# First block's attention: both maps' score products on 64-row halves of TensorE, written alternately, from one split of the queries

## The chip, the cores and the metric

The kernel runs on one core of a Trainium2 chip. The metric is the time of the whole program in device microseconds, a median over runs. The kernel before takes 3630.28 us (median of 3 runs).

## What is computed

The reference applies two transformer blocks of two layers each to 512 tokens of width 1024. The change touches one place: layer 0 of the first block, whose mixer is a differential attention over 8 heads. Each head has two maps (c = 0 and 1), each with queries and keys of width 64, and one set of values of width 128. The 512 latent tokens are the queries; the keys and values are those of 512 latent and 256 context tokens, 768 in all:

```python
def diff_attn_core(q, k, v, lam):
    s = jnp.einsum('bqhcd,bkhcd->bhcqk', q.astype(jnp.float32), k.astype(jnp.float32))
    p = jax.nn.softmax(s * (1.0 / math.sqrt(HEAD_DIM)), axis=-1)
    a = p[:, :, 0] - lam * p[:, :, 1]
    return jnp.einsum('bhqk,bkhe->bqhe', a.astype(v.dtype), v)
```

Each head's output is normed over its 128 channels and goes into the output product.

## The kernel before

The program is one long list of instructions for five engines. Its order on each engine is set when it is built, by a planner that lists instructions by its own estimates of when operands and buffers come free; on the chip each engine takes its list in order and waits with semaphores. All products with weights run in three passes: an operand is split into a high and a low part (float32r) that add up to it, and high x low, high x high and low x high are summed in PSUM (`mm3`, lines 246 to 254). Raw weights come by DMA into `wr`; the split (`split`, lines 221 to 223) writes the high part `wh` on ScalarE and the low part `wl` on VectorE, in 4 buffers each.

The attention stage, `diff_attention`, goes through 32 steps: 8 heads x 4 blocks of 128 queries (qi). QT[h] and KT[h] hold a head's queries and keys feature-major: 128 partitions, rows 0 to 63 for map 0 and 64 to 127 for map 1; columns are tokens (512 and 768). VV holds the values, token-major.

- `prep(h)` (named `after` and `psplit` inside, line 695 for all) makes a head's operands on GpSimd alone, one instruction after the other. `ks` is the pair of high and low keys. The high queries go into a `wh` buffer of the weights, twice: copy c is multiplied by a mask (`halves`) that is 0 on the other map's 64 rows. `qlo` is the low part of the queries.
- `scores(h, qi)` makes one map after the other. A map takes a PSUM tile `s` of two banks (768 columns used; three such tiles, s=3) and six products (line 723): the masked high queries against low and high keys, on all 128 rows, and the low queries against the high keys, on the map's 64 rows; each in a piece of 512 and one of 256 columns. Then VectorE takes the negative maximum over the keys (line 725), and ScalarE the exponential into `pp` with the row sum (line 727), which frees the tile.
- `mix(h, qi)`, one step later, joins the two maps on VectorE (lines 735 to 737), transposes the result on TensorE (line 746, tile `tr`, two banks) and copies it to `aT` on ScalarE (line 748).
- `values(h, half)` (line 757) multiplies with VV for two steps at a time; `finish_a` and `finish_b` sum squares (line 301), take the power on GpSimd (line 314), spread it (line 296), scale on VectorE (line 779) and split the head's output into `Oh` and `Ol`.

Ahead of the stage stands `qkv`, whose last products (the second half of the values) end in copies to VV on ScalarE (line 654). Behind it stands the output product with the weights `wo`.

Of the kernel before, what the change touches and what calls it, by code (L numbers as in the profile page):

```python
# [10 lines left out]
F32 = mybir.dt.float32  # L11
# [7 lines left out]
P = 128  # L19
# [9 lines left out]
# columns of the packed feature-major vectors  # L29
# [19 lines left out]
# columns of the packed row vectors  # L49
# [15 lines left out]
class Seg:  # L65
    """a run of tokens: columns lo..lo+w of x(k) for feature chunk k, columns off..off+w of the split activations"""
# [11 lines left out]
class Part:  # L78
    """tokens that share a PSUM bank in a product, and the segments that norms take one after the other"""
# [5 lines left out]
class Ps:  # L85
    """PSUM pool with a number of buffers per tag"""
# [8 lines left out]
class RmsMod:  # L95
    """rms norm with gain, scale and shift, into the split activations H"""
# [10 lines left out]
    def ahead(self, xn, seg, r=None):  # L107
        """normed values without gain and shift"""
        pr = self.net.row_bcast(self.sums(seg) if r is None else r)
        for k in range(KD):  # L110
            self.net.V.tensor_tensor(xn[:, k, seg.cols()], seg(k), pr, ALU.mult)
        self.early[seg.off] = xn
# [31 lines left out]
class LayerNorm:  # L144
    """layer norm of the stream in place, and its split in H (or each chunk handed to out)"""
# [27 lines left out]
class Net:  # L173
# [16 lines left out]
    def phase(self, ctx, name, tbufs, reuse="tile"):  # L190
        """open the scratch pool of a phase"""
        self.pool = ctx.enter_context(self.tc.tile_pool(name=self.nm(name), bufs=1, reuse_waits=reuse))
        self.tbufs = tbufs
# [20 lines left out]
    # ---- weights: raw float32 in, split into two float32r parts that add up to it  # L214
# [21 lines left out]
    def units(self, src, ks, n):  # L236
        """ks blocks of n columns, as many per unit as fit"""
# [8 lines left out]
    def mm3(self, outs, lhs, start, stop):  # L246
        """outs: list of (psum, rhs hi, rhs lo); lhs: (hi, lo)"""
# [13 lines left out]
    def later(self, steps, work):  # L261
        """have work done behind that many steps of products"""
        self.pending.append((self.steps + steps, work))

    def product(self, outs, lhs):
        """outs: list of (psum, k -> rhs hi, k -> rhs lo); lhs: list over k of (hi, lo)"""
# [4 lines left out]
    def constant(self, dst, rows, one, eng=None):  # L271
        """fill rows of a float32r tile [p, m, n] with 0 or 1"""
        (eng or self.G).memset(dst[rows].bitcast(F32), float(one))

    # ---- small vector arithmetic
# [17 lines left out]
    def bcast(self, dst, cols):  # L293
        """dst psum [128, 128*n]: row vector of cols[128 tok, n] on every partition"""
# [3 lines left out]
    def col_sums(self, dst, x):  # L298
        """dst psum [128 tok, n]: sums over the partitions of x [128, n*128 tok]"""
# [11 lines left out]
    def pow_half(self, dst, v):  # L311
        """dst = v ** -0.5 on GpSimd"""
# [17 lines left out]
    def row_ln(self, acc, accq, w, n):  # L330
        """rstd and mu*rstd per token, on every partition; sums over n channels"""
# [22 lines left out]
    # ---- setup  # L354
    def setup(self):
# [17 lines left out]
        self.halves = cp.tile([P, 2], F32, name="halves")  # L373
        nc.vector.memset(self.halves, 0.0)
        for c in range(2):
            nc.vector.memset(self.halves[64 * c:64 * c + 64, c:c + 1], 1.0)
# [17 lines left out]
    # ---- the nine modulation vectors of a layer, for one or both conditions  # L394
# [47 lines left out]
    def fill(self, n):  # L442
        """advance the pending modulation vectors by n steps"""
# [16 lines left out]
    def norm_scale(self, l, i, msc):  # L460
        """g * (1 + scale) for norm i of layer l: [128, 8, 2]"""
# [7 lines left out]
    # ---- product that ends in the stream: weights stationary, one unit list per chunk of output features.  # L469
    # The last chunks go segment by segment, so that the norm of one segment runs beside the product of the next.  # L470
# [21 lines left out]
    # ---- gated feed-forward on the split activations H  # L492
# [79 lines left out]
    # ---- first block, layer 0: differential attention  # L572
    def head_rope(self, pt, G, out, tabs):
        """pt psum [128, G*64] -> out: rms norm over 64, gain and rotation folded in the tables"""
# [18 lines left out]
    def rotate(self, src, cosg, sing, o3, q):  # L593
        """src [128, G, 4q]; pairs are (0,q), (2q,3q) blocks; sing holds -sin first, +sin second"""
# [11 lines left out]
    def rope_tables(self, cos, sin, g, w, tiles, scale=1.0):  # L606
        """cos [128, 4, w], sin signed; g [128, w]: tables with the gain folded in"""
# [21 lines left out]
    def qkv(self, H, QT, KT, VV):  # L629
        """queries and keys normed, rotated, feature-major; values token-major; context tokens are tiles 4 and 5"""  # L630
# [52 lines left out]
    def diff_attention(self, QT, KT, VV, O, keep):  # L683
        """O[h]: split feature-major outputs of head h. p0 - lam*s0/s1*p1 stands for the attention; the factor 1/s0 of
        each query goes into the norm over the head's channels: 1/s0 / sqrt(ms/s0^2 + eps) = 1/sqrt(ms + eps*s0^2)."""
# [5 lines left out]
        prev = []  # L691

        def after(*args):
            with self.tc.issue_after(prev.pop()) if prev else nullcontext():
                prev.append(G.tensor_tensor(*args).ins)

        def psplit(dst, src):
            one = self.ones[:, :1] if len(src.shape) == 2 else self.ones[:, :1].unsqueeze(1)
            after(dst[0], src, one.to_broadcast(list(src.shape)), ALU.mult)
            after(dst[1], src, dst[0].bitcast(F32), ALU.subtract)  # L700

        def prep(h):
            k = self.pair("ks", [P, NK], 2)
            psplit(k, KT[h])
            qh = self.wp.tile([P, 1024], F32R, name=self.nm("wh"), tag="wh", bufs=4).rearrange("p (c t) -> p c t", c=2)
            qlo = self.tile([P, T], "qlo", 2, F32R)
            for c in range(2):
                b = slice(64 * c, 64 * c + 64)
                after(qh[:, c], QT[h], self.halves[:, c:c + 1].to_broadcast([P, T]), ALU.mult)
                after(qlo[b], QT[h][b], qh[b, c].bitcast(F32), ALU.subtract)  # L710
            heads[h] = dict(qh=qh, qlo=qlo, k=k, s0=self.small(4, "s0", 3))

        def scores(h, qi):
            d = heads[h]
            ql = slice(qi * P, qi * P + P)
            d["p", qi], rr = [], (d["s0"][:, qi:qi + 1], self.small(1))
            for c in range(2):
                b = slice(64 * c, 64 * c + 64)
                st = self.bank("s", 1024)
                qh, qlo, (kh, kl) = d["qh"][:, c, ql], d["qlo"][b, ql], d["k"]  # L720
                for lh, r, on in ((qh, kl, (True, False)), (qh, kh, (False, False)), (qlo, kh[b], (False, True))):
                    for c0, c1 in ((0, 512), (512, NK)):
                        PE.matmul(st[:, c0:c1], lh, r[:, c0:c1], start=on[0], stop=on[1])
                nmax = self.small(1)
                V.tensor_reduce(nmax, st[:, :NK], axis=AX.X, op=ALU.max, negate=True)
                p = self.tile([P, NK], "pp", 6)
                S.activation(p, st[:, :NK], AF.Exp, bias=nmax, accum_out=rr[c])
# [73 lines left out]
    # ---- first block, layer 1: Fourier mix on half spectra  # L801
# [74 lines left out]
    # ---- second block  # L876
    def proj_tm(self, us, n, H, tt):
        """token-major product of token tile tt"""
# [12 lines left out]
    def mixer(self, l, H, norm):  # L891
# [19 lines left out]
        # attention operands per pair of heads: queries and keys feature-major, one head per block, then a row that  # L911
        # takes minus the maximum of each query (ones on the side of the keys); values token-major with ones between
# [604 lines left out]
```

## Time and profile before

| | |
|---|---|
| median of 3 runs (lowest, highest) | 3630.28 us (3626.2, 3633.18) |
| span of the profiled execution | 3633.2 us |
| TensorE products, busy share of the span | 94% |
| TensorE weight loads | 78% |
| VectorE | 57% |
| ScalarE | 35% |
| GpSimd | 14% |
| attention stage, first score product to first product with wo | 812.65 to 990.34 us |

The profiled execution's span lies at the upper end of the runs. Busy shares are means over stages that differ, so the stage is read for itself: a table of stretches gives the busy time of each engine in it, the waits say who ended whose idle time, and the timeline gives starts and durations. A product's duration in the timeline includes its way through the array, so products overlap in it; what a product costs in a row of products is the distance from start to start.

### The profile page before, as it was taken

How to read it: one execution, taken by the hardware profiler on the slowest of the kernel's cores; microseconds unless marked ns; L12 is line 12 of the kernel's file. 1: busy time of each engine (PE TensorE's matmuls, PEld its weight loads, DVE VectorE, ACT ScalarE, POOL GpSimd, SP SyncE). 2: the span in 40 equal slices, each digit the busy share in tenths (PEclk: the TensorE clock that was granted, in tenths of full speed). 3: DMA queues.
4: the chain of work that ended last, by engine and by line, in shares of the span. 5: the costliest groups of instructions: out<-in, count | busy, mean ns of one | idle time of the engine just before them, and what ended most of it. 6: DMA issues, size and time to landing. Idle time of an engine off the chain costs nothing.

```text
span 3633.2 us, 44413 instructions
## 1 busy us (share of the span) xinstructions
PE 3425.2 (94%) x17540; PEld 2839.1 (78%) x17540; DVE 2084.7 (57%) x3447; ACT 1267.5 (35%) x2180; POOL 517.0 (14%) x481
## 2 busy tenths in 40 slices
PE   7999999999999999999999999669999994999998
PEld 5888888777787778888888888557888873688887
DVE  6554355667664555333463336985744679666556
ACT  3211214336542224222452224235533441554333
POOL 1000001015410001000120003740100049020001
PEclk9999999999999999999999999879999996899999
DMA  6343352120045563333223333101333320023232
GB/s 222 122 141 112 101 161 72 50 70 1 24 154 160 181 195 123 99 95 97 74 99 93 93 98 91 41 21 47 93 95 97 93 80 14 18 70 110 90 102 64
DMA packets 99449, 341.80 MB, mean 94 GB/s; under 512 B 10916, under 2 KB 14116, under 8 KB 98984
## 3 DMA queue, kind: packets, MB, share of 16 engines
q1 hardware_dynamic: 99240, 338.96, 30.0%
q8 instruction: 138, 2.26, 0.3%
q14 instruction: 71, 0.58, 0.1%
HBM read 336.82 MB, written 2.10 MB: 93 GB/s over the span
## 4 chain that ended last, share of the span: by engine, by line
PE 35%; issue 6%; DVE 5%; POOL 4%; ACT 1%; ACTq 0%; DVEq 0%; POOLq 0%
PE mm L250 12%; PE mm L254 11%; PE mm L252 11%; POOL yb L1261 2%; POOL cx L1259 1%; DVE wl L223 1%; DVE ya L1255 0%; DVE s L290 0%; DVE s L291 0%; DVE s L289 0%; DVE t L164 0%; DVE t L165 0%; ACT H L222 0%; POOL s L314 0%; ACT X L166 0%
## 5 line engine op out<-in xcount | busy, mean ns | idle before, releaser
L222 ACT ACTIVATE wh<-wr 128x1024 fp32r<-128x1024 f32 (+4 forms) x505 | 510.9, 1014 | 1364.3 <-PE mm L252 894.2
L250 PE MATMUL mm<-H,wh 128*128 128x512 f32 (+1 forms) x2592 | 968.0, 374 | 11.6 <-DVE nm L1119 5.8
L254 PE MATMUL mm<-H,wl 128*128 128x512 f32 (+1 forms) x2592 | 963.0, 372 | 1.5 <-DVE wl L223 1.4
L252 PE MATMUL mm<-H,wh 128*128 128x512 f32 (+1 forms) x2592 | 964.2, 372 | 0.0
L223 DVE TENSOR_TENSOR wl<-wr,wh 128x1024 fp32r<-128x1024 f32 (+4 forms) x505 | 602.5, 1194 | 445.5 <-ACT wh L222 435.7
L250 PEld LDWEIGHTS mm<-H,wh 128*128 128x128 f32 x2592 | 494.6, 191 | 103.5 <-DVE nm L1119 6.5
L254 PEld LDWEIGHTS mm<-H,wl 128*128 128x128 f32 x2592 | 493.9, 191 | 85.8 <-DVE wl L223 2.3
L252 PEld LDWEIGHTS mm<-H,wh 128*128 128x128 f32 x2592 | 495.0, 191 | 83.5 <-issue 0.5
L254 PE MATMUL mm<-ah,wl 128*128 128x512 f32 (+1 forms) x1216 | 445.9, 367 | 0.0
L252 PE MATMUL mm<-ah,wh 128*128 128x512 f32 (+1 forms) x1216 | 443.8, 365 | 0.0
L250 PE MATMUL mm<-al,wh 128*128 128x512 f32 (+1 forms) x1216 | 443.1, 365 | 0.0
L252 PEld LDWEIGHTS mm<-ah,wh 128*128 128x128 f32 x1216 | 228.3, 188 | 42.4
L250 PEld LDWEIGHTS mm<-al,wh 128*128 128x128 f32 x1216 | 228.3, 188 | 42.3 <-issue 1.2
L254 PEld LDWEIGHTS mm<-ah,wl 128*128 128x128 f32 x1216 | 228.7, 188 | 39.5
L419 DVE SCALAR_TENSOR_TENSOR macc<-wr,SC,macc 128x1024 f32<-128x1024 f32 x133 | 168.3, 1281 | 94.3 <-DMA wr<-w_mod 93.7
L568 DVE SCALAR_TENSOR_TENSOR X<-mm,ng,X 128x512 f32<-128x512 f32 (+1 forms) x120 | 81.3, 678 | 244.8 <-PE mm L254 244.7
L314 POOL TENSOR_TENSOR s<-s,mhalf 128x2 f32<-128x2 f32 (+1 forms) x26 | 21.0, 806 | 1355.5 <-ACT s L321 816.4
L250 PE MATMUL mm<-wl,H 128*128 128x512 f32 (+2 forms) x480 | 180.7, 378 | 33.7 <-DVE wl L223 30.4
L528 DVE TENSOR_TENSOR act<-act,mm 128x512 f32<-128x512 f32 x88 | 60.3, 686 | 240.0 <-PE mm L254 239.8
L254 PE MATMUL mm<-wh,H 128*128 128x512 f32 (+2 forms) x480 | 176.7, 370 | 0.3
L252 PE MATMUL mm<-wh,H 128*128 128x512 f32 (+2 forms) x480 | 176.4, 368 | 0.0
L156 POOL TENSOR_TENSOR cx<-X 128x512 f32<-128x512 f32 x5 | 9.3, 1851 | 1005.7 <-DVE X L1267 638.2
(348 smaller groups left out, 4921.9 us busy)
## 6 DMA issues: line engine op xcount, KB each, us to landing
wr<-gu SPq DMA_DIRECT2D x176, 512.0 KB, 3.5
wr<-w_mod SPq DMA_DIRECT2D x136, 512.0 KB, 4.2
wr<-up SPq DMA_DIRECT2D x88, 512.0 KB, 3.5
wr<-dn SPq DMA_DIRECT2D x48, 448.0 KB, 3.4
wr<-down SPq DMA_DIRECT2D x32, 448.0 KB, 3.3
wr<-qkv SPq DMA_DIRECT2D x24, 512.0 KB, 4.3
wr<-dn SPq DMA_DIRECT2D x24, 512.0 KB, 3.6
wr<-w_out SPq DMA_DIRECT2D x16, 512.0 KB, 3.5
```

Source lines behind the costliest of these rows:

```text
L156: (net.G if k < KD - 1 else net.V).tensor_tensor(self.acc[:, sl], self.acc[:, sl] if k > 1 else seg(0), seg(k), ALU.add)
L222: self.S.activation(hi, src, AF.Copy)
L223: (eng or self.V).tensor_tensor(lo, src, hi.bitcast(F32), ALU.subtract)
L250: self.PE.matmul(pt, lh, rl, start=start, stop=False)
L252: self.PE.matmul(pt, lh, rh, start=False, stop=False)
L254: last = self.PE.matmul(pt, ll, rh, start=False, stop=stop)
L314: G.tensor_tensor(dst, v, self.mhalf.to_broadcast([P, w]), ALU.pow)
L419: self.V.scalar_tensor_tensor(acc[c], raw, s, acc[c], ALU.mult, ALU.add)
L528: self.V.tensor_tensor(to, to, pu, ALU.mult)
L568: self.V.scalar_tensor_tensor(s(d), pt, gate[0][:, d, s.cond:s.cond + 1], s(d), ALU.mult, ALU.add)
L1259: G.tensor_tensor(x, ap[:, j, t2:t2 + T], wt(t2).to_broadcast([P, T]), ALU.mult)
L1261: G.tensor_tensor(yb[:, j], yb[:, j], x, ALU.add)
```

## The change

The queries are split once, like any other operand: `split` with ScalarE for the high part and GpSimd for the low part, for keys and queries. `qs` is the new pair of queries, with two buffers of its own; the `wh` buffers, the masked copies and `halves` are not used any more. All six products of a map run on its 64 rows, and the code writes those of the two maps alternately, into two PSUM tiles taken together. Maxima and exponentials follow as before. The rest of the diff takes out comments and docstrings.

```diff
         def prep(h):
-            k = self.pair("ks", [P, NK], 2)
-            psplit(k, KT[h])
-            qh = self.wp.tile([P, 1024], F32R, name=self.nm("wh"), tag="wh", bufs=4).rearrange("p (c t) -> p c t", c=2)
-            qlo = self.tile([P, T], "qlo", 2, F32R)
-            for c in range(2):
-                b = slice(64 * c, 64 * c + 64)
-                after(qh[:, c], QT[h], self.halves[:, c:c + 1].to_broadcast([P, T]), ALU.mult)
-                after(qlo[b], QT[h][b], qh[b, c].bitcast(F32), ALU.subtract)
-            heads[h] = dict(qh=qh, qlo=qlo, k=k, s0=self.small(4, "s0", 3))
+            q, k = self.pair("qs", [P, T], 2), self.pair("ks", [P, NK], 2)
+            for dst, src in ((k, KT[h]), (q, QT[h])):
+                self.split(dst[0], dst[1], src, G)
+            heads[h] = dict(q=q, k=k, s0=self.small(4, "s0", 3))
 
         def scores(h, qi):
+
             d = heads[h]
             ql = slice(qi * P, qi * P + P)
             d["p", qi], rr = [], (d["s0"][:, qi:qi + 1], self.small(1))
+            st = [self.bank("s", 1024) for _ in range(2)]
+            half = [slice(64 * c, 64 * c + 64) for c in range(2)]
+            for i, (x, y) in enumerate(((0, 1), (0, 0), (1, 0))):
+                for c0, c1 in ((0, 512), (512, NK)):
+                    for c, b in enumerate(half):
+                        PE.matmul(st[c][:, c0:c1], d["q"][x][b, ql], d["k"][y][b, c0:c1], start=i == 0, stop=i == 2)
             for c in range(2):
-                b = slice(64 * c, 64 * c + 64)
-                st = self.bank("s", 1024)
-                qh, qlo, (kh, kl) = d["qh"][:, c, ql], d["qlo"][b, ql], d["k"]
-                for lh, r, on in ((qh, kl, (True, False)), (qh, kh, (False, False)), (qlo, kh[b], (False, True))):
-                    for c0, c1 in ((0, 512), (512, NK)):
-                        PE.matmul(st[:, c0:c1], lh, r[:, c0:c1], start=on[0], stop=on[1])
                 nmax = self.small(1)
```

The planner orders the instructions of the stage anew. Three places of the built orders follow; the number behind a name tells tiles apart.

ScalarE at the start of the stage, before: the last two VV copies of `qkv`, the table load and small exponential for lambda, then the first exponentials of head 0.

```order
L654 ACTIVATE VV<-mm_6784 128x512
L654 ACTIVATE VV<-mm_6810 128x512
L678 ACT_TABLE_LOAD
L678 ACTIVATE s_6846<-s_6846 128x2
L727 ACTIVATE pp_6877,s_6866<-s_6868,s_6875 128x768
```

The same place after:

```order
L650 ACTIVATE VV<-mm_6780 128x512
L222 ACTIVATE wh_8484<-wr_8482 128x1024
L222 ACTIVATE wh_8517<-wr_8515 128x1024
L222 ACTIVATE wh_8552<-wr_8550 128x1024
L650 ACTIVATE VV<-mm_6806 128x512
L222 ACTIVATE ks_6854<-KT_5124 128x768
L222 ACTIVATE qs_6852<-QT_5116 128x512
L674 ACT_TABLE_LOAD
L674 ACTIVATE s_6842<-s_6842 128x2
L222 ACTIVATE ks_6909<-KT_5125 128x768
L222 ACTIVATE qs_6907<-QT_5117 128x512
L222 ACTIVATE wh_8587<-wr_8585 128x1024
```

Four splits of wo units (wh from wr) have moved here from the last heads, and the high parts of head 0's and head 1's keys and queries stand here, those of head 0 behind the last VV copy.

TensorE in head 1, block 2, before: the two maps (tiles s_7121 and s_7132) follow one another, four products on 128 rows and two on 64 each.

```order
L723 MATMUL s_7121<-ks_6914,wh_6917 128x512
L723 MATMUL s_7121<-ks_6914,wh_6917 128x256
L723 MATMUL s_7121<-ks_6913,wh_6917 128x512
L723 MATMUL s_7121<-ks_6913,wh_6917 128x256
L723 MATMUL s_7121<-ks_6913,qlo_6918 128x512
L723 MATMUL s_7121<-ks_6913,qlo_6918 128x256
L723 MATMUL s_7132<-ks_6914,wh_6917 128x512
```

The same step after:

```order
L703 MATMUL s_7111<-ks_6910,qs_6907 128x512
L703 MATMUL s_7111<-ks_6910,qs_6907 128x256
L703 MATMUL s_7111<-ks_6909,qs_6907 128x512
L703 MATMUL s_7111<-ks_6909,qs_6907 128x256
L703 MATMUL s_7111<-ks_6909,qs_6908 128x512
L703 MATMUL s_7111<-ks_6909,qs_6908 128x256
L703 MATMUL s_7112<-ks_6910,qs_6907 128x512
```

All six products of map 0 (s_7111, upper 64 rows) still stand ahead of those of map 1 (s_7112, lower 64 rows), though the code alternates; every one is on 64 rows now.

TensorE in head 2, blocks 1 and 2, after: s_7257 and s_7258 are the maps of block 1, s_7313 and s_7314 those of block 2, tr_7246 is the spreading of a head's factor (line 296).

```order
L703 MATMUL s_7258<-ks_7079,qs_7077 128x512
L296 MATMUL tr_7246<-ident,or_7154 128x128 x4
L703 MATMUL s_7257<-ks_7079,qs_7077 128x256
L703 MATMUL s_7258<-ks_7079,qs_7077 128x256
L703 MATMUL s_7257<-ks_7079,qs_7078 128x512
L703 MATMUL s_7258<-ks_7079,qs_7078 128x512
L703 MATMUL s_7257<-ks_7079,qs_7078 128x256
L703 MATMUL s_7258<-ks_7079,qs_7078 128x256
L703 MATMUL s_7313<-ks_7080,qs_7077 128x512
L703 MATMUL s_7313<-ks_7080,qs_7077 128x256
```

TensorE in the same head before, from the second map of block 0 (s_7231) to the first of block 1 (s_7267):

```order
L723 MATMUL s_7231<-ks_7085,qlo_7090 128x512
L757 MATMUL tr_7210<-aT_7100,VV 128x256 x6
L723 MATMUL s_7231<-ks_7085,qlo_7090 128x256
L723 MATMUL s_7267<-ks_7086,wh_7089 128x512
L723 MATMUL s_7267<-ks_7086,wh_7089 128x256
```

In the order after, the alternation is kept here, and both maps of block 1 end within one product of each other; before, the maps follow one another, and the six products of a map stand between the end of one and the end of the next.

## Rows read from the trace of the kernel before

**Rows 1.** Stretches: window, us, busy us (instructions) of PE, PEld, DVE, ACT, POOL, clock, DMA

```profile
850.00:890.00 40.00, 39.92 (x197) 28.86 (x196) 29.85 (x41) 24.49 (x57) 21.10 (x21) 1.00 0.00 1
```

**Rows 2.** Groups, 812 to 972 us: operation, count | busy us, mean ns | idle before

```profile
L737 DVE SCALAR_TENSOR_TENSOR pp<-pp,s,pp 128x768 f32<-128x768 f32 x29 | 36.2, 1247 | 0.4
...
L695 POOL TENSOR_TENSOR qlo<-QT,wh 64x512 fp32r<-64x512 f32 x15 | 23.3, 1556 | 1.2
...
L736 DVE SCALAR_TENSOR_TENSOR s<-s,nlam,s 128x1 f32<-128x1 f32 x29 | 17.6, 606 | 0.3
...
L695 POOL TENSOR_TENSOR wh<-QT,halves 128x512 fp32r<-128x512 f32 x15 | 16.5, 1101 | 0.0
...
L695 POOL TENSOR_TENSOR ks<-KT,ones 128x768 fp32r<-128x768 f32 x7 | 10.3, 1467 | 39.2 <-PE s L723 39.1
L223 POOL TENSOR_TENSOR Ol<-t,Oh 128x512 fp32r<-128x512 f32 x6 | 7.7, 1279 | 18.9 <-ACT Oh L222 18.9
```

**Rows 3.** Timeline of TensorE in a burst of maps: start, us, operation, count

```profile
837.85 0.96 PE L723 MATMUL s<-ks,wh 128*128 128x512 f32 x4
838.74 0.61 PE L723 MATMUL s<-ks,qlo 64*128 64x512 f32 x2
839.28 0.96 PE L723 MATMUL s<-ks,wh 128*128 128x512 f32 x4
```

**Rows 4.** Timeline of TensorE, 512- and 256-column products alternating

```profile
300.13 0.40 PE L250 MATMUL mm<-H,wh 128*128 128x512 f32 x1
...
300.49 0.40 PE L252 MATMUL mm<-H,wh 128*128 128x512 f32 x1
...
301.19 0.40 PE L250 MATMUL mm<-H,wh 128*128 128x512 f32 x1
```

**Rows 5.** Timeline of GpSimd, TensorE and ScalarE around the start

```profile
783.99 1.83 POOL L695 TENSOR_TENSOR ks<-KT,ks 128x768 fp32r<-128x768 f32 x1
...
812.65 0.85 PE L723 MATMUL s<-ks,wh 128*128 128x512 f32 x4
812.85 0.60 ACT L654 ACTIVATE VV<-mm 128x512 f32<-128x512 f32 x1 [4.84 <-PE mm L254]
```

**Rows 6.** Waits, 812 to 972 us: who, for whom, us, times, longest

```profile
DVE s L725 <- PE s L723: 33.6, 29, 5.0
...
PEld s L723 <- issue: 24.6, 102, 0.7
...
PEld s L723 <- ACT pp L727: 1.2, 3, 0.7
```

**Rows 7.** Timeline of TensorE, VectorE and ScalarE in the last burst

```profile
965.94 0.75 DVE L779 SCALAR_TENSOR_TENSOR t<-t,subg,tr 128x512 f32<-128x512 f32 x1 [0.57 <-PE tr L296]
966.72 0.63 ACT L222 ACTIVATE Oh<-t 128x512 fp32r<-128x512 f32 x1 [0.33 <-DVE t L779]
967.30 0.61 PE L723 MATMUL s<-ks,qlo 64*128 64x512 f32 x2
967.95 0.96 DVE L725 TENSOR_REDUCE s<-s 128x1 f32<-128x768 f32 x1 [0.32 <-PE s L723]
968.82 0.21 DVE L736 SCALAR_TENSOR_TENSOR s<-s,nlam,s 128x1 f32<-128x1 f32 x1
968.94 0.90 ACT L727 ACTIVATE pp<-s,s 128x768 f32<-128x768 f32 x1 [0.36 <-DVE s L725]
970.27 1.01 DVE L737 SCALAR_TENSOR_TENSOR pp<-pp,s,pp 128x768 f32<-128x768 f32 x1
```

**Rows 8.** Timeline, then a stretch, at the stage's end

```profile
974.13 1.20 DVE L223 TENSOR_TENSOR wl<-wr,wh 128x1024 fp32r<-128x1024 f32 x1
...
989.93 0.65 PE L296 MATMUL tr<-ident,or 128*128 128x128 f32 x4 [1.63 <-POOL or L314]
990.34 0.48 PE L250 MATMUL mm<-Ol,wh 128*128 128x512 f32 x1
...
992.00:994.00 2.00, 2.00 (x6) 1.59 (x5) 0.00 (x0) 0.13 (x1) 1.27 (x1) 0.50 0.00 0
```

More of the change, by code (lines that the diff above doesn't have):

```diff
@@ L372, in setup @@
             nc.vector.memset(t, e)
-        self.halves = cp.tile([P, 2], F32, name="halves")
-        nc.vector.memset(self.halves, 0.0)
-        for c in range(2):
-            nc.vector.memset(self.halves[64 * c:64 * c + 64, c:c + 1], 1.0)
         self.SC = cp.tile([P, KD, 32], F32, name="SC")
@@ L689, in diff_attention @@
         heads = {}
[L691 to L700, printed above, removed]
-        def prep(h):
-            k = self.pair("ks", [P, NK], 2)
-            psplit(k, KT[h])
-            qh = self.wp.tile([P, 1024], F32R, name=self.nm("wh"), tag="wh", bufs=4).rearrange("p (c t) -> p c t", c=2)
-            qlo = self.tile([P, T], "qlo", 2, F32R)
-            for c in range(2):
-                b = slice(64 * c, 64 * c + 64)
-                after(qh[:, c], QT[h], self.halves[:, c:c + 1].to_broadcast([P, T]), ALU.mult)
-                after(qlo[b], QT[h][b], qh[b, c].bitcast(F32), ALU.subtract)
-            heads[h] = dict(qh=qh, qlo=qlo, k=k, s0=self.small(4, "s0", 3))
+        def prep(h):
+            q, k = self.pair("qs", [P, T], 2), self.pair("ks", [P, NK], 2)
+            for dst, src in ((k, KT[h]), (q, QT[h])):
+                self.split(dst[0], dst[1], src, G)
+            heads[h] = dict(q=q, k=k, s0=self.small(4, "s0", 3))
         def scores(h, qi):
@@ L716, in scores @@
             d["p", qi], rr = [], (d["s0"][:, qi:qi + 1], self.small(1))
-            for c in range(2):
-                b = slice(64 * c, 64 * c + 64)
-                st = self.bank("s", 1024)
-                qh, qlo, (kh, kl) = d["qh"][:, c, ql], d["qlo"][b, ql], d["k"]
-                for lh, r, on in ((qh, kl, (True, False)), (qh, kh, (False, False)), (qlo, kh[b], (False, True))):
-                    for c0, c1 in ((0, 512), (512, NK)):
-                        PE.matmul(st[:, c0:c1], lh, r[:, c0:c1], start=on[0], stop=on[1])
+            st = [self.bank("s", 1024) for _ in range(2)]
[4 more added lines that the diff above has]
+                        PE.matmul(st[c][:, c0:c1], d["q"][x][b, ql], d["k"][y][b, c0:c1], start=i == 0, stop=i == 2)
+            for c in range(2):
                 nmax = self.small(1)
-                V.tensor_reduce(nmax, st[:, :NK], axis=AX.X, op=ALU.max, negate=True)
+                V.tensor_reduce(nmax, st[c][:, :NK], axis=AX.X, op=ALU.max, negate=True)
                 p = self.tile([P, NK], "pp", 6)
-                S.activation(p, st[:, :NK], AF.Exp, bias=nmax, accum_out=rr[c])
+                S.activation(p, st[c][:, :NK], AF.Exp, bias=nmax, accum_out=rr[c])
                 d["p", qi].append(p)
```

## Prediction

> **What bounds the kernel now.** I read the table of stretches first: from 812 us to 972 us, the score stage of the first block's attention, TensorE is busy 39.92 of 40 us (850 to 890 stands for the four stretches) while VectorE is at 29.85, ScalarE at 24.49 and GpSimd at 21.10 [rows 1]. So this stage is TensorE's, and a microsecond taken from TensorE there is a microsecond of the kernel, until VectorE (three quarters busy) or a wait takes its place. The waits say the same: VectorE's largest, 33.6 us, is for the score products; TensorE's largest has no releaser, 24.6 us in 102 pieces called "issue" at the scores' weight loads; its wait for a score bank (the exponentials of line 727 give banks back) is 1.2 us in all [rows 6].
>
> What are the 102 pieces? The timeline of TensorE answers. One map of one step is six products: four on 128 rows (wh, against the low and high keys), two on 64 rows (qlo). The four start at 837.85, the two at 838.74, the next map's four at 839.28: 0.89 + 0.54 = 1.43 us a map [rows 3]. Where 512- and 256-column products alternate without a change of rows, six take 300.13 to 301.19 = 1.06 us [rows 4]. The difference, 0.37 us, is two changes between 128-row and 64-row mode: **0.185 us a change**, in which the engine drains and the first load is not hidden. This is the price that the change attacks.
>
> **Part by part.** *Fewer mode changes.* In the new kernel all score products use 64 rows; transposes, values and sums use 128. I counted in the built instruction orders, from the first score product to the last product of the stage: 154 changes of mode before, 107 after (a transpose put between two 128-row products used to be free and now costs two changes, so not all 128 go). 47 x 0.185 = **-8.7 us**, all of it on TensorE's path.
>
> *Alternation.* The code asks for twelve products per step that alternate between the halves. The order does not keep it: of 32 steps, only 8 alternate in a lasting way (step 0 with 11 changes of half, five steps with 8, two with 3 or 4); in the other 24 all six products of map 0 stand ahead of map 1's, since the second bank comes late. In all 95 neighbours change half, 235 stay on one. No row of the trace has two neighbouring products on different halves (the two qlo groups of a step are always parted by wh products), so the price is bounded by the nearest rows: at best each change of half hides a 256-column product, 300.49 - 300.13 = 0.36 us a pair, of which a third is the 256 columns, 0.12 us, so -11.4 us; at worst it costs as much as a mode change, +17.6 us. I take **-2 us**: some overlap, most of it lost because in the same steps TensorE waits (next point). The Trainium skill ("TensorE: Matmul & The Clock Gate", Part 3) says that products on different row groups run at once, about 4 ns apart; by that rule this term is the whole -11.4, and it is my second rival.
>
> *Where alternation survives, a bank is late.* There are three score banks. Before, map 0 ends 1.43 us ahead of map 1, so its maximum and exponential run beside map 1's products. In the 8 alternating steps both maps end together. The next step's map 0 takes the third bank (1.06 us); its map 1 needs the bank of the old map 0: maximum 0.96 us and exponential 0.90 us later, and about 0.1 us for the handovers (products end 967.30 + 0.61 = 967.91, maximum at 967.95 to 968.91, exponential at 968.94) [rows 7] = 1.96 us, so TensorE stands 0.9 us. In five of the eight the broadcast product and its VectorE operation (0.75 us, line 779 [rows 7]) stand just ahead of that maximum, which adds up to 0.3 us. 8 x 1.1 = **+9 us**, against 1.2 us of such waits now [rows 6]. The Trainium skill ("TensorEngine Tiling (Array Packing)", PSUM Bottleneck) warns of just this, that packing speeds up TensorE and not the emptying of PSUM. Bounds: 0, if the other work between hides it, to 8 x 1.96 = 15.7.
>
> *The start.* Before, GpSimd makes head 0's operands without ScalarE: the low keys end at 783.99 + 1.83 and the first score starts at 812.65, straight behind the last projection product [rows 5]. After, ScalarE makes the high parts, and its order puts head 0's ks and qs copies behind the last VV copy, which waits for that last product: it ends at 812.85 + 0.60 = 813.45. Then the 128x768 copy (no such row; the exponential of that size takes 0.90), then the low keys on GpSimd, 1.83 with VectorE idle: 813.45 + 0.90 + 1.83 = 816.2, and one handover. First score 3.6 us later than now, and the low queries (a subtraction of this size takes GpSimd 1.28, the Ol row [rows 2]) hold the last four products until 817.5. I take **+3.8 us**; below 3.0 it can't be, since copy and subtraction are in line.
>
> *Behind the start.* A weight unit's split (1.20 us on VectorE [rows 8]) that stood in the last heads now stands between the second and third maximum, and the second head's two copies ahead of the first exponential. So maps 4 and 6 wait for banks: **+2 us** (0 to 3). TensorE's idle time can also cost clock: at the stage's end it waits 1.63 us, and 992 to 994 runs at 0.50 of the clock (1.2 GHz) [rows 8]. Such a stretch at the new start would fall in waits for banks: **+0.5 us** (0 to 1.7).
>
> *ScalarE and GpSimd.* ScalarE gets 8 x (0.90 + 0.63) = 12.2 us more (the 512-column copy is the Oh row [rows 7]): 24 of 40 us become 27, still far from the bound. GpSimd loses the ones- and halves-products: per head 1.47 + 2 x 1.10 + 2 x 1.56 go, one subtraction of 1.28 comes [rows 2]. That helps VectorE: the p update takes 1.247 on average but 1.01 in a burst with GpSimd idle, the small factor 0.606 against 0.21 [rows 2, 7]. I count nothing for it: VectorE waits for TensorE 33.6 us; at best it trims the bank waits by 2 us. The wh buffers that qh no longer holds let four splits of the next stage go early; the loads' order is the same, and the next stage starts behind the same chain at the tail: nothing.
>
> **Sum**: -8.7 - 2 + 9 + 3.8 + 2 + 0.5 = **+4.6 us**. The profiled execution spans 3633.2 us, at the upper end of the three runs (3626.2 to 3633.18); 3633.2 + 4.6 = 3637.8 in it, and against the median of 3630.28: **3635 us**. One effect, a shift of the free phase of the clock's dips later on, I can't sum: +-2 us.
>
> **Rivals.** *1. A change of half costs like a change of mode* (slower). For it: nothing in the trace shows two halves at work at once. Then +17.6 in place of -2; the slower TensorE hides about 5 us of the bank waits: 4.6 + 19.6 - 5 = +19, 3649 us. It decides from about 0.05 us a change of half on, where 95 x 0.05 + 2 brings the sum above +7.3. *2. Full overlap and hidden waits* (faster): -8.7 - 8 - 0, with 3 of the 9 us of waits, 3.8 and 0: -10, 3620 us. For it: VectorE has 11 us of 40 free, and GpSimd disturbs it less. Against: with both maps ready at once the bank chain of 1.96 us is longer than the one map that covers it. By the rule of the TensorE page named above this is what the tiles would allow. *3. No overlap and no price*: the halves simply follow one another; 4.6 + 2 = +6.6, 3637 us. *4. The clock*: the 3.6 us gap at the start and the waits behind it hold TensorE at 1.2 GHz for longer than one such stretch; twice 1.7 us for it and once more at the tail, +5 on top: 3640 us. That the change does not do what it says is partly built in: 24 of 32 steps don't alternate.
>
> **How the numbers follow.** About 0.2% (7.3 us) is what a measurement of this kernel can tell from no change: 3623.0 to 3637.5 is "same". Forecast 0.42 (its own range 3629 to 3639; 0.37 same, 0.05 slower); rival 1 0.15 (slower); rival 2 0.15 (0.12 faster, 0.03 same); rival 3 0.17 (0.10 same, 0.07 slower); rival 4 0.11 (0.09 slower, 0.02 same). Faster 0.12, same 0.52, slower 0.36. Range 3620 to 3648: it leaves out the far half of rival 1 and what lies beyond rival 2.
>
> **What would show it.** First score product about 816.3 us, not 812.65, with TensorE's wait put on GpSimd. "Issue" at the scores' loads down by about a third. A map that follows on the same half at 1.06 us, not 1.43. In alternating steps, starts of neighbours a few ns to 0.1 us apart (overlap), 0.12 to 0.22 (none) or 0.3 and more (rival 1). Waits of score loads on the exponentials: from 1.2 to about 10 us in the stage; if they stay near 2, rival 2 holds. The stage from 812.65 to the first wo product at 990.34 (177.7 us) [rows 5, 8] should come out at about 182. I am wrong if ScalarE gets at head 0's copies before the last VV copy, or if the bank waits hide under values and transposes.

## The result, and the profile after

The changed kernel takes **3674.47 us** (median of 4 runs, 3673.49 to 3677.72) against 3631.73 for the kernel before on the same chip (4 runs, 3626.2 to 3633.94): ratio 1.0117, 95% interval 1.0104 to 1.0129. It is slower by some 43 us; the forecast was 3635 us, with a range up to 3648. The profiled execution spans 3675.9 us, so the difference to the profiled one of before (3633.2) is 42.7 us as well, and it can be split by three times in the two traces: the first score product, the first product with wo, the end.

| | before | after | difference |
|---|---|---|---|
| up to the first score product | 812.65 | 814.01 | +1.4 |
| from there to the first product with wo | 177.7 | 196.9 | **+19.2** |
| from there to the end of the span | 2642.9 | 2665.0 | **+22.1** |

So there are two losses, one in the stage that was changed and one, just as large, in code that was not touched.

**The stage.** The table of stretches of after, with the columns of [rows 1] (us; busy us and instructions of TensorE, its loads, VectorE, ScalarE, GpSimd; clock; DMA):

```profile
812.00:850.00 38.00, 34.09 (x146) 26.45 (x147) 27.30 (x40) 26.68 (x55) 13.98 (x11) 0.66 0.11 42
850.00:890.00 40.00, 37.70 (x176) 27.86 (x176) 18.75 (x31) 20.06 (x47) 8.13 (x11) 0.85 0.00 0
890.00:930.00 40.00, 35.42 (x186) 26.99 (x185) 26.64 (x39) 24.86 (x56) 12.27 (x14) 0.91 0.00 1
930.00:972.00 42.00, 38.50 (x191) 28.96 (x190) 25.68 (x41) 24.41 (x55) 9.32 (x11) 0.88 0.00 1
972.00:990.00 18.00, 16.88 (x85) 12.39 (x85) 7.43 (x13) 9.62 (x23) 1.21 (x2) 0.85 0.00 1
990.00:1010.00 20.00, 17.23 (x88) 13.74 (x84) 7.34 (x14) 8.84 (x22) 4.87 (x8) 0.88 0.00 1
```

The column to look at is the clock. Before it is 1.00 from 812 to 990 [rows 1]; after it is 0.66 in the first stretch and 0.85 to 0.91 behind it, up to the stage's end at 1010.94. It is a mean of two levels, 2.4 and 1.2 GHz: the engine ran at half speed for two thirds of 812 to 850 us (0.66 = 1 - 0.68/2) and for parts of every stretch. Summed over the rows, (1 - clock) x us is 12.9 + 6.0 + 3.6 + 5.0 + 2.7 + 2.4 (the rows are rounded), some **32 us** of full-speed time lost; before, nothing in the stage.

The waits of the same stage (who, for whom, us in total, times, longest), which answer to [rows 6]:

```profile
DVE s L706 <- PE s L703: 30.3, 16, 6.3
PEld s L703 <- ACT pp L708: 9.5, 8, 1.5
PEld s L703 <- issue: 7.4, 38, 0.3
PE s L703 <- ACT pp L708: 6.9, 7, 1.2
PE s L703 <- POOL ks L223: 3.3, 1, 3.3
```

"Issue" at the score loads fell from 24.6 us in 102 pieces to 7.4 in 38: most of these pieces are gone, as intended, though the order still has 107 of the 154 mode changes. Waits for a PSUM tile rose from 1.2 to 9.5 us (the second line; the fourth tells them from the products' side), and one wait of 3.3 us stands at the start. The timeline of ScalarE, GpSimd and TensorE there, which answers to [rows 5] (start, duration, engine, line, operation):

```profile
811.24 0.83 ACT L222 ACTIVATE ks<-KT 128x768 fp32r<-128x768 f32 x1
```

```profile
812.16 1.80 POOL L223 TENSOR_TENSOR ks<-KT,ks 128x768 fp32r<-128x768 f32 x1 [175.16 <-DMA wr<-wo]
```

```profile
810.32 0.40 PE L254 MATMUL mm<-wh,H 128*128 128x512 f32 x1
814.01 4.20 PE L703 MATMUL s<-ks,qs 64*128 64x512 f32 x18 [3.30 <-POOL ks L223]
```

GpSimd's subtraction for the low keys starts when ScalarE's copy of the high keys has ended (811.24 + 0.83 = 812.07), so that copy is what it waited for; the DMA that the row names brings weights of `wo`, which it doesn't read.

VectorE's and GpSimd's groups answer to [rows 2] (count | busy us, mean ns):

```profile
L718 DVE SCALAR_TENSOR_TENSOR pp<-pp,s,pp 128x768 f32<-128x768 f32 x27 | 32.0, 1185 | 0.5
L717 DVE SCALAR_TENSOR_TENSOR s<-s,nlam,s 128x1 f32<-128x1 f32 x27 | 11.3, 420 | 0.2
L223 POOL TENSOR_TENSOR qs<-QT,qs 128x512 fp32r<-128x512 f32 x8 | 10.2, 1276 | 40.1 <-ACT qs L222 40.1
```

With less work on GpSimd the p update takes 1185 ns instead of 1247 and the small factor 420 instead of 606. It buys nothing, since neither engine is the bound.

**The rest of the program.** Behind the stage both kernels have the same instructions in the same order, and the clock is 1.00 in both at the places compared. Yet the distance between the two traces grows steadily. A stretch of the first block's later layer, all products with weights, before and then after (the same place of the program):

```profile
1590.00:1690.00 100.00, 100.00 (x437) 81.85 (x436) 34.66 (x37) 25.23 (x30) 0.00 (x0) 1.00 0.31 98
```

```profile
1616.00:1716.00 100.00, 100.00 (x430) 80.38 (x429) 34.63 (x37) 25.27 (x30) 0.00 (x0) 1.00 0.30 92
```

TensorE is busy all the time in both, at full clock, and starts 437 products in 100 us before, 430 after: 1.6% fewer. From start to start a 512-column product that moves H takes 227 ns before and 233 after. Their group from 1500 to 2900 us shows 5 ns more in the mean duration, before and after:

```profile
L250 PE MATMUL mm<-H,wh 128*128 128x512 f32 x972 | 381.3, 392 | 3.1 <-DVE nm L1119 3.0
```

```profile
L250 PE MATMUL mm<-H,wh 128*128 128x512 f32 x973 | 386.7, 397 | 3.1 <-DVE nm L1100 3.1
```

### The profile page after: what moved, and what is told of

Same layout as the page of the kernel before. It is cut to its first block, busy times and chain, and to the rows that moved or that the text cites. A ratio compares the mean times of both kernels' runs of the same rounds, so it can differ in the third digit from the quotient of the medians.

```text
span 3675.9 us, 44399 instructions
## 1 busy us (share of the span) xinstructions
PE 3455.0 (94%) x17540; PEld 2840.8 (77%) x17540; DVE 2072.4 (56%) x3444; ACT 1276.7 (35%) x2196; POOL 470.8 (13%) x449
## 4 chain that ended last, share of the span: by engine, by line
PE 36%; issue 6%; DVE 4%; POOL 4%; ACT 1%; POOLq 0%; ACTq 0%; DVEq 0%
PE mm L250 12%; PE mm L254 11%; PE mm L252 11%; POOL yb L1242 2%; POOL cx L1240 1%; DVE wl L223 1%; DVE ya L1236 0%; DVE s L290 0%; DVE s L291 0%; DVE s L289 0%; ACT H L222 0%; ACT X L166 0%; DVE t L164 0%; PE tr L296 0%; POOL s L314 0%
## 5 line engine op out<-in xcount | busy, mean ns | idle before, releaser
L250 PE MATMUL mm<-H,wh 128*128 128x512 f32 (+1 forms) x2592 | 973.7, 376 | 10.4 <-DVE nm L1100 3.3
L222 ACT ACTIVATE ah<-act 128x512 fp32r<-128x512 f32 (+1 forms) x132 | 88.0, 667 | 162.2 <-DVE act L552 110.0
```

Source lines behind the costliest of these rows:

```text
L222: self.S.activation(hi, src, AF.Copy)
L250: self.PE.matmul(pt, lh, rl, start=start, stop=False)
```

## The experiments

Two questions: why do products far from the change take longer, and why does the clock fall in the stage?

### Addresses: the small tile that went

The diff takes out `halves`, 8 bytes per partition. It occupied 32 bytes in the middle of the constants, and every tile that is allocated behind it (weights, scratch pools, values) stands 32 bytes lower in the changed kernel; H, allocated from the other end, does not move. Three kernels move tiles and nothing else, with each engine's order kept.

`a_pad`, the changed kernel with the 32 bytes put back:

```diff
-        self.mhalf = cp.tile([P, 1], F32, name="mhalf")
+        self.mhalf = cp.tile([P, 9], F32, name="mhalf")[:, :1]
```

> The changed kernel, every engine's order unchanged; the one column of the constant mhalf gets eight unused columns behind it, so that all tiles behind it stand 32 bytes further, where they stood in the kernel before (there the tile halves filled these 32 bytes). Theory A, addresses: behind the attention stage the traces drift apart by some 22 us at a full clock in both, because products that move H against wh (233 ns apart instead of 227) read from other addresses. The drift then goes: about 3652 us, with the attention stage still near 197 us, or somewhat less if addresses bear on it too. Theory B, something else that the change brings (the other pools, weights already in place, the power state behind the stage): 3674 us, products 233 ns apart as before.

Measured: 3653.88 us (3642.34 to 3659.36), ratio to before 1.0053 (1.0032 to 1.0074). The stretch that answers to those above:

```profile
1612.00:1712.00 100.00, 100.00 (x437) 81.85 (x437) 35.97 (x40) 26.25 (x32) 0.00 (x0) 1.00 0.31 95
```

437 products again, and from the first wo product to the end of the trace's products 2633.3 us against 2632.1 before and 2654.3 after. The stage is still long, 201.2 us (the traced execution is the slowest of the four).

`b_shift`, the kernel before with `halves` tucked into unused bytes behind `mhalf`, so that all the rest moves down by 32 bytes:

```diff
-        self.mhalf = cp.tile([P, 1], F32, name="mhalf")
+        mh = cp.tile([P, 3], F32, name="mhalf")
+        self.mhalf, self.halves = mh[:, :1], mh[:, 1:]
...
-        self.halves = cp.tile([P, 2], F32, name="halves")
```

> The kernel before, every engine's order unchanged; the mask halves moves into unused bytes behind mhalf, so that all tiles behind it stand 32 bytes lower, as in the changed kernel. Theory A, addresses: about 3654 us, with products of H and wh 233 ns apart behind the attention stage and the stage itself at 178 us with the clock at full speed. If addresses make the stage slow as well, up to 3674. Theory B: 3631 us, products 227 ns apart.

Measured: 3662.03 us (3657.81 to 3666.47), ratio 1.0080 (1.0065 to 1.0095), some 29 us slower for a move of 32 bytes. The stage is 177.7 us as before, so addresses have no part in its loss; the products have:

```profile
1598.00:1698.00 100.00, 100.00 (x431) 80.39 (x430) 34.65 (x37) 25.25 (x30) 0.00 (x0) 1.00 0.30 93
```

Theory A holds from both sides: put back, the loss behind the stage goes; taken out alone, it comes. What about an address matters? My guess was the place within 64 bytes. Two runs on the kernel before asked that.

`b_all64` (`mhalf` of 17 columns: everything behind it but H 64 bytes further) and `b_pools32` (tiles of tag `s0` 32 bytes longer: only the scratch pools, with al, ah and VV, move, by 96 bytes):

```diff
-        self.mhalf = cp.tile([P, 1], F32, name="mhalf")
+        self.mhalf = cp.tile([P, 17], F32, name="mhalf")[:, :1]
```

```diff
-        return self.sp.tile([P, 8], F32, ...
+        return self.sp.tile([P, 16 if tag == "s0" else 8], F32, ...
```

> The kernel before, every order unchanged; mhalf gets 16 unused columns, so that all tiles behind it except H stand 64 bytes further. If the place within 64 bytes is what counts, nothing changes: 3633 us, products of H and wh 227 ns apart. If the distance to H or another place counts, up to 3662, products 233 ns apart.

> The kernel before, every order unchanged; the tiles of tag s0 are made 32 bytes longer each, three of them, so that all pools behind the small one (al, ah, VV, the keys) stand 96 bytes further, while weights and H stay. If products run at 227 ns where stationary and moving tile stand alike within 64 bytes, and 231 to 237 ns otherwise, the some 2500 products of 512 columns that move al and ah against wh win 5 to 9 ns each: 10 to 20 us, about 3618 us. If the offset within 64 bytes isn't what counts, 3633 or more.

Measured: `b_all64` 3658.58 us, ratio 1.0070 (1.0055 to 1.0085); `b_pools32` 3630.71 us, ratio 0.9999 (0.9988 to 1.0010). The guess fell twice. After 64 bytes the place within 64 is the old one, and the products are as slow as after 32:

```profile
1591.00:1691.00 100.00, 100.00 (x431) 80.52 (x430) 34.58 (x38) 24.73 (x30) 0.00 (x0) 1.00 0.29 95
```

And in `b_pools32` the 256-column products that move al and ah went from 118 to 120 ns down to 113 or 114, while those of 512 columns came to 233 (before: 231 to 237). In its trace the rest of the program is 7.0 us shorter than before, the stage 2.8 us and the part ahead of it 5.7 us longer, so that nothing is left in the median; why the part ahead is longer is not shown. So the addresses of the two operands set a product's pace, within about 3% at 512 columns and 6% at 256, and which relation between them is the good one stays open.

### The clock: rows, alternation or waits

`a_pad_maps` and `a_pad_gprep` undo one part each of the change (on `a_pad`, so that addresses stay those of before). The first writes the six products of one map, then those of the other:

```diff
-            for i, (x, y) in enumerate(((0, 1), (0, 0), (1, 0))):
-                for c0, c1 in ((0, 512), (512, NK)):
-                    for c, b in enumerate(half):
+            for c, b in enumerate(half):
+                for i, (x, y) in enumerate(((0, 1), (0, 0), (1, 0))):
+                    for c0, c1 in ((0, 512), (512, NK)):
```

The second splits keys and queries on GpSimd alone, in a chain, as the kernel before did:

```diff
-                self.split(dst[0], dst[1], src, G)
+                one = self.ones[:, :1].to_broadcast(list(src.shape))
+                after(dst[0], src, one, ALU.mult)
+                after(dst[1], src, dst[0].bitcast(F32), ALU.subtract)
```

> As a_pad, but the score products are written map by map instead of alternately, all still on 64 rows. If alternation (both halves at once, later maxima, bank waits) is what makes the granted clock fall and the stage long, the stage returns toward the kernel before with fewer mode changes: about 170 to 178 us, 3631 to 3625 with A holding. If products on 64 rows as such, or the gap at the start, lower the clock, the stage stays at 193 to 198 us and the time near a_pad.

> As a_pad, but keys and queries are split by GpSimd alone in a chain, as the kernel before made them; nothing of head 0 waits behind the last copy of VV, so the gap of 3.3 us ahead of the first score goes. If that gap is what starts the low clock, the 20 us at 1.2 GHz behind it go too, the stage is shorter by 3 + 8 to 10 us, and by more if the later dips hang on the first: a_pad minus 11 to 20. If the score products themselves lower the clock, only the gap goes: a_pad minus 3, with the low stretches in about the same total.

Measured: 3657.63 us (ratio 1.0052, 1.0028 to 1.0077) and 3650.71 us (1.0050, 1.0035 to 1.0065); `a_pad` had 1.0053. Neither part undone brings the time back. The six executions of `a_pad_maps` lie far apart, 3641.92 to 3666.39 us, with a mean clock from 0.964 to 0.956; the traced one is the slowest, with a stage of 208.9 us and a clock of 0.59 to 0.83 in its stretches. In `a_pad_gprep` the first score follows the last projection product at once (815.32, 815.63), the gap of 3.3 us is gone, and the clock falls all the same:

```profile
812.00:850.00 38.00, 32.12 (x139) 24.75 (x138) 28.41 (x38) 21.20 (x41) 12.38 (x9) 0.69 0.17 56
850.00:890.00 40.00, 37.00 (x183) 27.07 (x182) 26.72 (x37) 22.43 (x53) 17.05 (x17) 0.86 0.00 1
```

That leaves the 64 rows. `b_rows64` is the kernel before with the high products on the map's own 64 rows (the mask makes the others zero). Orders, addresses, GpSimd's masked copies: all as before.

```diff
-                for lh, r, on in ((qh, kl, (True, False)), (qh, kh, (False, False)), (qlo, kh[b], (False, True))):
+                for lh, r, on in ((qh[b], kl[b], (True, False)), (qh[b], kh[b], (False, False)), (qlo, kh[b], (False, True))):
```

`b_rows128` goes the other way: the low queries, too, stand in tiles whose other 64 rows are zeroed once, and all six products run on 128 rows.

```diff
+        qlos = [self.tile([P, 2, T], f"qlo{i}", 1, F32R) for i in range(2)]
+        for t in qlos:
+            for c in range(2):
+                self.constant(t[:, c], slice(64 - 64 * c, 128 - 64 * c), 0)
...
-            qlo = self.tile([P, T], "qlo", 2, F32R)
+            qlo = qlos[h % 2]
...
-                after(qlo[b], QT[h][b], qh[b, c].bitcast(F32), ALU.subtract)
+                after(qlo[b, c], QT[h][b], qh[b, c].bitcast(F32), ALU.subtract)
...
-                qh, qlo, (kh, kl) = d["qh"][:, c, ql], d["qlo"][b, ql], d["k"]
-                for lh, r, on in (..., (qlo, kh[b], (False, True))):
+                qh, qlo, (kh, kl) = d["qh"][:, c, ql], d["qlo"][:, c, ql], d["k"]
+                for lh, r, on in (..., (qlo, kh, (False, True))):
```

> The kernel before, with one change: the products of the high queries run on the map's own 64 rows instead of 128 (the mask makes the other 64 rows zero, so the sums are the same). Every engine's order, every address and every wait stay. Theory C, rows: products on 64 rows are what lowers the granted clock of the attention stage; then the clock falls here too, though nothing alternates and no gap stands at the start: some 20 to 35 us of clock lost in the stage, against 10 to 20 us won by mode changes that go, and the time is 3638 to 3655 us. Rival D, alternation and waits: without them the clock stays at full speed and the mode changes that go are a gain: the stage 160 to 172 us instead of 178, 3615 to 3627 us.

> The kernel before, with the low queries masked as the high ones are (each map's copy stands in a tile whose other 64 rows are zeroed once), so that all six score products run on 128 rows and no product of the stage changes between 64 and 128 rows. Theory C: the granted clock stays at full speed and the 154 mode changes of 0.185 us go: up to 28 us, the stage 150 to 160 us, 3605 to 3615 us, less where VectorE's maxima or the PSUM tiles set the pace instead (3615 to 3628). Rival D says nothing against it; if the mode change costs nothing, 3631 to 3635.

Measured: `b_rows64` 3641.67 us (10 runs, 3632.78 to 3645.57), ratio 1.0023 (1.0014 to 1.0032), stage 186.9 us. `b_rows128` **3614.56 us** (3611.64 to 3619.72), ratio 0.9953 (0.9936 to 0.9969), stage 167.3 us: faster than both kernels. Of the 21.2 us by which its trace is shorter than that of before, 10.4 stand in the stage; the other 6.1 ahead of it and 4.7 behind it stand where TensorE's order is the same, and ahead of it the clock was higher (1.00 against 0.91 in the first 100 us), so the change of rows is not shown to be their cause. The stretches of `b_rows64`, then of `b_rows128`:

```profile
812.00:850.00 38.00, 35.12 (x153) 26.81 (x152) 23.46 (x33) 19.22 (x41) 22.02 (x19) 0.73 0.00 0
850.00:890.00 40.00, 39.13 (x191) 29.11 (x192) 26.59 (x35) 21.75 (x52) 22.56 (x21) 0.87 0.00 1
890.00:930.00 40.00, 38.56 (x199) 29.15 (x196) 30.45 (x41) 24.11 (x56) 23.49 (x21) 0.91 0.00 1
930.00:972.00 42.00, 40.55 (x209) 30.03 (x208) 31.98 (x43) 27.92 (x61) 18.76 (x18) 0.89 0.11 38
972.00:990.00 18.00, 16.15 (x80) 12.13 (x78) 12.79 (x24) 11.48 (x25) 2.73 (x3) 0.87 0.03 5
```

```profile
812.00:850.00 38.00, 34.42 (x193) 28.00 (x192) 31.41 (x41) 24.73 (x57) 24.16 (x21) 1.00 0.00 1
850.00:890.00 40.00, 38.15 (x220) 31.53 (x219) 33.22 (x43) 26.46 (x61) 24.62 (x22) 1.00 0.00 1
890.00:930.00 40.00, 36.18 (x203) 29.73 (x202) 34.65 (x43) 25.34 (x59) 26.45 (x22) 0.96 0.08 27
930.00:972.00 42.00, 39.27 (x229) 33.08 (x227) 26.64 (x43) 29.16 (x66) 9.04 (x11) 0.99 0.07 26
```

Compare 850 to 890. With 64 rows TensorE is busy 39.13 of 40 us and the clock is 0.87; with 128 rows it is busy less, 38.15, and the clock is 1.00. Idle time is not what separates them: `b_rows128` waits more over its stage (14 us against 11). From before to `b_rows64` only the rows of four products in six differ, and the clock goes from 1.00 to between 0.73 and 0.91. Theory C is shown; D falls.

The falls themselves say the same. The clock of `b_rows64` falls six times in the stage. The first and longest (823.2 to 843.7, 10 of the 26 us lost) stands behind a wait of 2.2 us for a tile, so idle time may have begun it. In the 4 us ahead of each of the other five TensorE is busy 3.61 to 4.00 us. The stretches ahead of one such fall, in it, and in the first:

```profile
877.20:881.20 4.00, 4.00 (x25) 2.88 (x23) 3.96 (x3) 1.71 (x5) 3.92 (x3) 1.00 0.00 0
881.20:884.60 3.40, 3.40 (x14) 2.45 (x14) 1.18 (x3) 1.75 (x4) 3.24 (x6) 0.51 0.00 0
823.20:843.70 20.50, 20.50 (x68) 15.34 (x67) 14.94 (x18) 9.81 (x22) 11.49 (x10) 0.50 0.00 0
```

One thing the runs don't part: wherever the high products run on 64 rows, products on the two halves also overlap (below), so whether the rows alone lower the clock, or rows with this overlap, is open.

`a_gprep_maps` (`a_pad_gprep`, map by map) is the same thing from the other side: the changed kernel without its gap, its alternation and its addresses.

> As a_pad_gprep, map by map, nothing written alternately; against the kernel before, the only differences are the 64 rows of the high products and the missing masked copies, so it should read as b_rows64 does: 3638 to 3646 us, 25 to 30 us of clock lost in the stage (theory C). If alternation has a part in the fall of the clock or in the length of the stage, it stands 5 us or more below a_pad_gprep, 3650.7.

Measured: 3646.43 us (5 runs, 3637.74 to 3647.88), ratio 1.0039 (1.0025 to 1.0053), stage 186.7 us against 186.9 in `b_rows64`. It reads as that kernel does, as C expects; that alternation costs something can't be told from the times (1.0039 against 1.0050, intervals overlapping), though the stage is 194.1 us with it.

Would both halves at work at once keep the clock? `a_gprep_alt` holds all twelve products of a step in strict alternation, where the changed kernel's order does so in a few steps:

```diff
-                        PE.matmul(st[c][:, c0:c1], ...
+                        with self.tc.issue_after(last) if last else nullcontext():
+                            last = PE.matmul(st[c][:, c0:c1], ...).ins
```

> As a_pad_gprep, but the twelve score products of a step are held in strict alternation between the two halves, in all 32 steps (in the changed kernel only some steps alternate in the built order). The halves of a step then run at once: about 1.1 us of products less a step, up to 35 us over the stage, against waits for the third PSUM tile of about 1 us a step. Theory C as it stands (products on 64 rows lower the clock, whether one half works or both): the clock still falls, and the waits add idle time: stage 185 to 200 us, 3640 to 3655 us. Rival E: with both halves at work the whole array is busy, so the clock holds; then the stage is 150 to 170 us and the time 3605 to 3625 us.

Measured: 3693.68 us (3684.33 to 3695.68), ratio 1.0172 (1.0155 to 1.0189), stage 234.1 us: the slowest of all, outside what either theory expected. Its stretches, and its largest waits of TensorE and VectorE:

```profile
819.00:860.00 41.00, 25.23 (x128) 17.72 (x127) 25.85 (x36) 19.48 (x41) 11.54 (x9) 0.67 0.15 50
860.00:900.00 40.00, 32.64 (x156) 23.82 (x155) 21.52 (x31) 18.54 (x43) 12.29 (x13) 0.76 0.00 1
```

```profile
DVE s L717 <- PE s L713: 72.2, 25, 5.3
PE s L713 <- ACT pp L719: 36.9, 17, 5.7
```

E's forecast fails: the clock is 0.67 to 0.87 over the whole stage. But its idea isn't settled, for here 64 rows and waits come together (TensorE is busy 32.64 of 40 us), so this run doesn't tell how much of its clock is due to which. The waits are those that the prediction described: both maps end together, their maxima and exponentials follow one after the other, and there are three tiles.

## Why the prediction was wrong, point by point

**Mode changes, -8.7: right in kind, and the price inside a map holds.** In `b_rows128` all 154 are gone, and its maps follow one another at 1.04 and 1.06 us (806.54, 807.58, 808.64), where before they took 1.43 [rows 3]:

```profile
806.54 0.85 PE L728 MATMUL s<-ks,wh 128*128 128x512 f32 x4
...
807.58 0.87 PE L728 MATMUL s<-ks,wh 128*128 128x512 f32 x4
...
808.64 0.86 PE L728 MATMUL s<-ks,wh 128*128 128x512 f32 x4
```

As a mean over all 154 the price comes out lower. The stage is 10.4 us shorter, lost 2 us of clock (0.04 x 40 + 0.01 x 42) and waits 10 us more than before (14.3 against 4.4): 22 us less work, 0.14 us a change instead of 0.185 (an estimate, which counts waits and lost clock as lost in full).

**Alternation, -2: mis-sized, and not where I looked for it.** Halves do run at once, and the order needn't alternate for it. In `b_rows64` the maps stand one after another in TensorE's order, six products each (wh, wh, wh, wh, qlo, qlo), neighbouring maps on different halves. This is what it did with the first three (start, duration, operation and form of the first, count):

```profile
816.15 0.96 PE L723 MATMUL s<-ks,wh 64*128 64x512 f32 x5
816.95 0.39 PE L723 MATMUL s<-ks,qlo 64*128 64x512 f32 x1
816.95 0.50 PE L723 MATMUL s<-ks,wh 64*128 64x256 f32 x2
817.19 0.28 PE L723 MATMUL s<-ks,qlo 64*128 64x256 f32 x1
817.30 0.40 PE L723 MATMUL s<-ks,wh 64*128 64x256 f32 x2
817.42 0.39 PE L723 MATMUL s<-ks,qlo 64*128 64x512 f32 x1
817.54 0.28 PE L723 MATMUL s<-ks,wh 64*128 64x256 f32 x1
817.65 0.28 PE L723 MATMUL s<-ks,qlo 64*128 64x256 f32 x1
817.66 0.51 PE L723 MATMUL s<-ks,wh 64*128 64x512 f32 x2
818.01 0.51 PE L723 MATMUL s<-ks,qlo 64*128 64x512 f32 x2
```

Map 0's two qlo products start at 816.95 and 817.19. Ahead of the second, seven wh products have been started (five and two), and map 0 has four: three are map 1's, which stand behind that qlo product in the order. So TensorE does not take its list strictly in order, as the description of the kernel before has it for every engine. Eighteen products take 818.01 + 0.51 - 816.15 = 2.37 us; at 1.06 us a map they would take 3.18 [rows 4]. So places where two maps meet can gain, not only the 95 neighbours that I counted, and by the following estimate my lower bound of -11.4 was none. `b_rows64` without its lost clock is 161 us (186.9 - 26 from its five rows), with 6.8 us more waits for tiles than before (7.2 against 0.4), that is 23 us less work. The 47 mode changes that it has less (107, as the changed kernel) are 6.6 of it at 0.14, and the rest, some 17 us, I put down to this overlap; no run has the one without the other. The Trainium skill ("TensorE: Matmul & The Clock Gate", Part 3) has products on different row groups start about 4 ns apart, where the trace agrees (864.387 and 864.391 in the changed kernel); it also says there that products start and end strictly in program order, and here the trace differs. Rival 1, a change of half as dear as a change of mode, falls.

**Tile waits, +9 in 8 steps: right in size.** TensorE waits for the exponential 8 times, 8.0 us in all from 812 to 1010, the longest 1.2. But such waits don't need the alternation: `b_rows64`, whose order has one map behind the other, waits 8 times too, 7.2 us.

**Start, +3.8: right in mechanism and size.** 3.30 us behind the low keys on GpSimd. The first score comes at 814.01 and not 816.3 only because the last projection product started 2.1 us earlier (810.32 against 812.42).

**Behind the start, +2: not seen.** The one wait for a tile there is 0.15 us, at 818.37. The clock stood at 0.50 from 814.1 to 834.4, so what it would be at full clock is not shown.

**Clock, +0.5 with rival 4 at +5: the step that failed in the stage.** I asked only what idle time could do to the clock, because the one row at half clock stood behind a wait [rows 8]. That the products themselves, on 64 rows instead of 128, could lower it I did not ask. It cost some 32 us. Taken as lost in full (an estimate), the stage without it is 196.9 - 32 = 165 us, 13 below the 177.7 of before with the tile waits in it; my own terms for the stage (-8.7 - 2 + 9 + 2) gave +0.3. So the array work that the change saves was more than I counted, and the clock took it back about two and a half times over.

**The rest of the program, "nothing" and +-2: the step that failed there.** I costed every instruction that the change removes and none of the bytes. 22 us came from a tile of 8 bytes: products that move H are 233 ns apart instead of 227, and 21 us of the 22 go when the bytes are put back (`a_pad`).

**What would show it.** "Issue" fell by 70%, not by a third. Score loads wait 9.5 us for the exponentials, as said. The stage is 196.9, not 182. Both signs of failure named there (ScalarE's order at the start, hidden waits) were the wrong ones to watch.

## What to carry to other kernels

Before you cut a matmul's rows to what holds data, ask what the clock does: here rows of zeros took no time, and filling the last third of the products up to 128 rows made the stage 10 us shorter, while cutting the others down to 64 cost more than the mode changes that it saved. When a trace drifts at full clock, in the same order, far from the edit, compare the distance from start to start of a common product and then the addresses; hold them fixed (pad what you remove) before you judge any change of this size. A packing by rows that stands block after block overlapped by itself here; one that makes two results ready at once needs the buffers, and the engines behind them, for two.

## What was not expected of the hardware

- The granted clock of TensorE went with the rows in use: 0.87 with 64-row score products at 39.13 of 40 us busy, 1.00 with 128-row ones at 38.15.
- A product's pace depends on where its operands stand: 227 or 233 ns from start to start for 512 columns of H, 113 to 120 for 256 columns of al and ah, by moves of 32 to 96 bytes. A move of 32 bytes alone cost 29 us (0.8%) of the program.
- TensorE starts products of the next map on the free half ahead of products of this map that stand before them in its order: three maps in 2.37 us instead of 3.18.
